# A hybrid decoder layer: the SSD's normed rows are written to a PSUM bank of their own

## The chip, the cores and the metric

The kernel runs on one core of one Trainium2 chip. The metric is the device time of one execution in microseconds (us); lower is better. Five engines work side by side, each through its own instructions in order: TensorE (PE in the profile; its weight loads are PEld), VectorE (DVE), ScalarE (ACT), GpSimd (POOL), and SyncE (SP), which here issues the DMAs. They wait for each other by semaphores.

## The reference

The layer is one decoder block over 2048 tokens of width 1024. Its first half feeds two mixers from one input projection, and the SSD mixer's tail is what the change touches:

```python
proj = u @ w_in[i]
q, k, v, qi, ki, wi, z, xbc, dt = jnp.split(proj, offsets, axis=-1)
attn = sparse_attention(q, k, v, qi, ki, wi, rel_bias)   # top-256 keys per query
ssd = ssd_mixer(z, xbc, dt, conv_w[i], conv_b[i], dt_bias[i], a_log[i], d_skip[i], ssd_norm_w[i])
mix = jnp.concatenate([attn, ssd], axis=-1) @ w_out[i]
h = h + rms_norm(mix, norm_post_mix[i])
f = rms_norm(h, norm_pre_mlp[i]) @ w_mlp_up[i]
f = jnp.square(jax.nn.relu(f)) @ w_mlp_down[i]
h = h + rms_norm(f, norm_post_mlp[i])

# the end of ssd_mixer: y is (tokens, 512), in 2 groups of 256
y = y * jax.nn.silu(z)
yg = y.reshape(Bn, L, 2, 256)
yg = yg * lax.rsqrt(jnp.mean(yg * yg, axis=-1, keepdims=True) + EPS)
y = yg.reshape(Bn, L, 512) * norm_w
```

## The kernel before

Tokens go in four tiles `t` of 512, each of four chunks `c` of 128. Large products are made from high and low parts: each operand is split into a rounded part and a remainder, and `mm3` (L255) issues three matmuls for one (L257, L260, L261). These are the main products: the input projection into `p_mm` (`in_proj`, 21 products of 24 matmuls for each tile), then for each tile the output projection into `p_acc` and the MLP into `p_mm` and `p_dn`.

The program has a front (input projection of the four tiles) and then four windows, one for each tile (output projection and MLP). Beside the main products run the side tasks: the top-k search of the sparse attention (`topk`), the attention itself (`attention`), and the SSD (`ssd`). `weave` (L934) interleaves them in the text by given start and end points, with a priority for each kind. The order on each engine is then made by a scheduler that plays the program through by its own estimates and takes the most urgent instruction that it finds ready; so one added instruction or one other buffer can move what comes after it, on every engine.

`ssd(t)` walks the chunks in order, for two groups `g` of heads in each. `enter(c, g)` loads the tile `si` (three buffers), transposes it into `p_x` (L496, L497) and makes the decays `lm` and `cb`: after `p_x` come DVE's L500, ACT's L502 and DVE's L503, and only then can the chunk's matmuls start. `carry` issues these into `p_y` (L514, L515) and `p_st` (L517), and updates the state. `leave(c, sis)` normalizes the two groups of a finished chunk: squares (L530), sums of squares by matmuls into `p_ms` (L532), the reciprocal root on DVE (`rsqrt`), and for each group a matmul that spreads the result over a bank's columns (L538, into the same bank `p_ms`). DVE multiplies it into the rows (L540, two instructions of 128 columns), ACT makes the high part (L542), DVE the low part (L543), and SP stores both to `mix_d`, from which the output projection reads.

A chunk's order in the text is: carry of group 0 (`p_y`, `p_st`), enter of group 1 (`p_x`), carry of group 1 (`p_y`, `p_st`), enter of the next chunk's group 0 (`p_x`), and leave (`p_ms`). For the first three tiles these take turns on two PSUM banks, `acc` and `acd` (`rings["acc"]`, L100): each call of `pt` takes the other bank, and waits until the earlier tile in it is done with. The transposes and spreads of the input projection (`p_tr` at L341 and L422, `p_rs` at L288) take turns on the same two. The fourth tile's SSD uses the three banks `tp`, which it shares with top-k and attention.

Of the kernel before, what the change touches and what calls it, by code (L numbers as in the profile page):

```python
# [8 lines left out]
F32 = mybir.dt.float32  # L9
# [6 lines left out]
AF = mybir.ActivationFunctionType  # L16
OP = mybir.AluOpType
# [24 lines left out]
def hybrid_layer(ctx, tc, x, x_t, w_cols, n_post_mix, n_post_mlp, w_in, w_misc, dt_bias, a_log, d_skip,  # L42
                 w_out, w_up, w_down, rel_bias, c_ident, c_flip, c_stack, c_tri, c_trineg, c_caus, c_bucket, out, dbg=None):
    nc = tc.nc
    V, S, G, PE, SP = nc.vector, nc.scalar, nc.gpsimd, nc.tensor, nc.sync
# [56 lines left out]
    def pt(tag, name=None):  # L102
        pool, bufs, slot = place(tag)
        return pool.tile([P, 512], F32, tag=slot, name=name or tag, bufs=bufs)
# [27 lines left out]
    w_pm, w_pl, w_ssd = cols[:, 0:8], cols[:, 8:16], cols[:, 56:60]  # L132
# [69 lines left out]
    def rsqrt(o, v, n, scale, who="s", work=None, also=None):  # L202


        if work is None:
            xx, u = (tl(who, [P, n], name=name) for name in ("rs_x", "rs_u"))
        else:
            xx, u = work[:, 0:n], work[:, n:2 * n]
        yi = tl(who, [P, n], I32, name="rs_y")
        V.tensor_scalar(xx, v, scale, EPS, op0=OP.mult, op1=OP.add)  # L210
        if also is not None:
            V.scalar_tensor_tensor(xx, also, scale, xx, op0=OP.mult, op1=OP.add)
        V.tensor_scalar(yi, xx.bitcast(I32), -0.5, float(0x5f3759df), op0=OP.mult, op1=OP.add)
        y = yi.bitcast(F32)
        q = tl(who, [P, n], name="rs_q")

        V.tensor_tensor(u, xx, y, op=OP.mult)
        V.tensor_tensor(u, u, y, op=OP.mult)
        V.tensor_scalar(q, u, 0.375, -1.25, op0=OP.mult, op1=OP.add)
        V.tensor_tensor(u, u, q, op=OP.mult)  # L220
        V.scalar_tensor_tensor(y, u, 1.875, y, op0=OP.add, op1=OP.mult)

        V.tensor_tensor(u, xx, y, op=OP.mult)
        V.scalar_tensor_tensor(u, u, -0.5, y, op0=OP.mult, op1=OP.mult)
        V.scalar_tensor_tensor(o, u, 1.5, y, op0=OP.add, op1=OP.mult)
# [232 lines left out]
    def ssd(t):  # L458
        bank = "acc" if t < NT - 1 else "tp"
# [65 lines left out]
        def leave(c, sis):  # L525

            p = pt(bank, "p_ms")
            for g, si in enumerate(sis):
                ys, sq = si[:, 0:2], si[:, 2:4]
                S.activation(sq, ys, AF.Square)  # L530
                for j in range(2):
                    PE.matmul(p[:, g:g + 1], sq[:, j], cn["ones"], start=j == 0, stop=j == 1)  # L532
            rs = tl("ssm", [P, 2], name="rs_s")
            rsqrt(rs, p[:, 0:2], 2, 1.0 / 256, "ssm", p[:, 2:6])
            for g, si in enumerate(sis):
                ys, yp = si[:, 0:2], si[:, 2:6].rearrange("p (s j) t -> p s j t", s=2).bitcast(F32R)
                sl = slice((g + 1) * P, (g + 2) * P)
                PE.matmul(p[:, sl], rs[:, g:g + 1].broadcast_to([P, P]), ident, start=True, stop=True)  # L538
                for j in range(2):
                    V.scalar_tensor_tensor(ys[:, j], ys[:, j], w_ssd[:, 2 * g + j:2 * g + j + 1], p[:, sl],  # L540
                                           op0=OP.mult, op1=OP.mult)
                S.activation(yp[:, 0], ys, AF.Copy)  # L542
                V.tensor_tensor(yp[:, 1], ys, yp[:, 0].bitcast(F32), op=OP.subtract)  # L543
                r0, t0 = 512 + 256 * g, t * T + c * P
                for s in range(2):
                    SP.dma_start(mix_d[s, r0:r0 + 256, t0:t0 + P].rearrange("(j p) t -> p j t", p=P), yp[:, s].bitcast(F32))
# [541 lines left out]
```

## Time and profile before

| | |
|---|---|
| three runs | 2923.69, 2925.88, 2927.11 us; median 2925.88 us |
| the profiled execution | 2928.29 us, its span 2926.5 us |
| share of the span that an engine is busy | PE 94%, POOL 60%, DVE 56%, ACT 51% |
| mean granted TensorE clock | 0.973 of full speed |
| the front, 0 to 895 us | PE busy 789.28 us of 895, granted clock 0.94 |
| the rest, 895 to 2926 us | PE busy 1972.61 us of 2031, granted clock 0.99 |

How to read it: a busy PE is not PE at its peak, since matmuls overlap; but an idle PE is time in which it had nothing that it could start. The granted clock is the share of full speed that TensorE was given. The SSD's leaves lie between 189 and 881 us, so all that the change edits runs in the front and at the start of the first window.

### The profile page before, as it was taken

The page shows a single profiled execution, that of the slowest core. Times are in us where ns is not written, and L with a number is a line of the kernel's source. Part 1 is how long each engine was busy: PE and PEld are TensorE (multiplying, and loading weights), DVE is VectorE, ACT ScalarE, POOL GpSimd, SP SyncE. Part 2 cuts the span into 40 slices and gives each one's busy share as a digit, 9 for nine tenths or more (in the row PEclk, how much of TensorE's full clock was granted, in tenths as well). Part 3 has the DMA queues.
Part 4 walks back from the last instruction along what each step waited for, and adds up shares of the span by engine and source line. Part 5 has one row for each costly group of instructions (what it writes and reads, how often), then busy time and mean ns, then how long its engine had stood idle before and what let it go on. Part 6 is the DMA issues. An engine that isn't in the chain of part 4 may idle for free.

```text
span 2926.5 us, 41201 instructions
## 1 busy us (share of the span) xinstructions
PE 2761.9 (94%) x13558; PEld 2250.7 (77%) x13558; DVE 1642.4 (56%) x4106; ACT 1481.5 (51%) x2550; POOL 1762.6 (60%) x1721
## 2 busy tenths in 40 slices
PE   7988989789989999998999999999999999999998
PEld 5766767667768887887787888878888888778886
DVE  5479588888575666747765565666444342511113
ACT  2375477675837575677773847644332332311101
POOL 4666556667666656654456575644564656588775
PEclk8999989999989999999999999999999999999999
DMA  3765654634733333255223222553222225522222
GB/s 128 224 189 151 218 157 149 208 118 160 249 120 119 112 103 102 90 176 180 101 94 98 90 97 79 170 177 102 87 95 81 93 78 177 204 95 97 95 94 86
DMA packets 286741, 383.46 MB, mean 131 GB/s; under 512 B 26520, under 2 KB 151360, under 8 KB 286528
## 3 DMA queue, kind: packets, MB, share of 16 engines
q1 hardware_dynamic: 286528, 380.84, 40.0%
q8 instruction: 107, 1.75, 0.2%
q14 instruction: 106, 0.87, 0.1%
HBM read 316.44 MB, written 64.30 MB: 130 GB/s over the span
## 4 chain that ended last, share of the span: by engine, by line
PE 67%; DVE 13%; ACT 6%; DMA 5%; issue 4%; POOL 3%; SPq 1%; POOLq 0%; DVEq 0%; ACTq 0%
PE p_mm L257 9%; PE p_mm L261 9%; PE p_mm L260 9%; PE p_dn L260 7%; PE p_dn L261 7%; PE p_dn L257 7%; ACT junk_k L610 5%; PE p_o L725 4%; PE p_s L683 4%; PE p_pt L717 3%; POOL wl L232 2%; PE p_ix L591 1%; DVE cnd L618 1%; PE p_acc L260 1%; PE p_acc L257 1%
## 5 line engine op out<-in xcount | busy, mean ns | idle before, releaser
L232 POOL TENSOR_TENSOR wl<-wr,wh 128x512 fp32r<-128x512 f32 (+1 forms) x740 | 987.0, 1335 | 179.6 <-ACT wh L229 107.0
L231 POOL TENSOR_SCALAR wh<-wr 128x512 fp32r<-128x512 f32 x674 | 449.6, 667 | 752.1 <-PE p_mm L260 372.8
L257 PE MATMUL p_mm<-u,wh 128*128 128x512 f32 (+1 forms) x1696 | 685.4, 404 | 47.4 <-ACT u L311 15.4
L261 PE MATMUL p_mm<-u,wl 128*128 128x512 f32 (+1 forms) x1696 | 682.8, 404 | 13.2 <-POOL wl L232 12.9
L260 PE MATMUL p_mm<-u,wh 128*128 128x512 f32 (+1 forms) x1696 | 674.9, 398 | 0.6 <-POOL u L309 0.3
L610 ACT ACTIVATE junk_k<-sc,cnd 128x512 int8<-128x512 f32 (+10 forms) x434 | 576.4, 1328 | 157.8 <-DVE cnd L618 122.2
L257 PEld LDWEIGHTS p_mm<-u,wh 128*128 128x128 f32 (+1 forms) x1696 | 322.9, 190 | 119.3 <-ACT u L311 17.5
L260 PE MATMUL p_dn<-wl,g 128*128 128x512 f32 x1008 | 402.2, 399 | 4.2 <-POOL wl L232 4.2
L261 PE MATMUL p_dn<-wh,g 128*128 128x512 f32 x1008 | 399.5, 397 | 2.7 <-POOL g L836 2.7
L261 PEld LDWEIGHTS p_mm<-u,wl 128*128 128x128 f32 (+1 forms) x1696 | 322.5, 190 | 88.7 <-POOL wl L232 21.3
L260 PEld LDWEIGHTS p_mm<-u,wh 128*128 128x128 f32 (+1 forms) x1696 | 322.6, 190 | 69.6 <-DVE u L312 2.3
L257 PE MATMUL p_dn<-wh,g 128*128 128x512 f32 x1008 | 328.0, 398 | 1.9 <-POOL wh L231 1.3
L834 ACT ACTIVATE r<-r 128x512 f32<-128x512 f32 x128 | 80.4, 629 | 437.1 <-DVE r L833 436.7
L688 DVE CUSTOM_DVE_ANT_0 pp<-p_s,mk 128x512 f32<-128x512 f32 (+3 forms) x320 | 192.5, 607 | 134.3 <-PE p_s L683 130.5
L719 ACT ACTIVATE ppt<-p_pt 128x512 fp32r<-128x512 f32 (+1 forms) x288 | 155.3, 568 | 208.1 <-PE p_pt L717 170.0
L720 DVE TENSOR_TENSOR ppt<-p_pt,ppt 128x512 fp32r<-128x512 f32 (+1 forms) x288 | 182.6, 655 | 129.6 <-ACT ppt L719 126.9
L260 PEld LDWEIGHTS p_dn<-wl,g 128*128 128x128 f32 x1008 | 190.3, 189 | 46.8 <-POOL wl L232 5.5
L261 PEld LDWEIGHTS p_dn<-wh,g 128*128 128x128 f32 x1008 | 190.3, 189 | 43.8 <-POOL g L836 3.1
L257 PEld LDWEIGHTS p_dn<-wh,g 128*128 128x128 f32 x1008 | 185.8, 189 | 42.0 <-POOL wh L231 2.9
L725 PE MATMUL p_o<-ppt,VV 128*128 128x256 f32 x1088 | 211.1, 294 | 1.9 <-DVE ppt L720 1.0
L617 DVE TENSOR_SCALAR keep<-cnt 128x1 int32<-128x1 f32 (+1 forms) x341 | 70.2, 206 | 244.1 <-ACT junk_k L610 242.7
L836 POOL TENSOR_TENSOR g<-r,g 128x512 fp32r<-128x512 f32 x128 | 170.1, 1331 | 53.2 <-ACT g L835 51.9
(253 smaller groups left out, 4177.6 us busy)
## 6 DMA issues: line engine op xcount, KB each, us to landing
wr<-w_up SPq DMA_DIRECT2D x256, 256.0 KB, 2.6
wr<-w_down SPq DMA_DIRECT2D x256, 256.0 KB, 2.6
wr<-w_in SPq DMA_DIRECT2D x160, 256.0 KB, 2.9
tq<-toep_d SPq DMA_DIRECT2D x128, 128.0 KB, 2.6
qs<-q_d SPq DMA_DIRECT2D x256, 64.0 KB, 2.5
wr<-w_out SPq DMA_DIRECT2D x64, 256.0 KB, 3.7
mix<-mix_d SPq DMA_DIRECT2D x32, 512.0 KB, 8.1
q_d<-qp SPq DMA_DIRECT2D x24, 512.0 KB, 3.6
```

Source lines behind the costliest of these rows:

```text
L231: G.tensor_scalar(dst_hi, src_f, 1.0, 0.0, op0=OP.mult, op1=OP.add)
L232: G.tensor_tensor(dst_lo, src_f, dst_hi.bitcast(F32), op=OP.subtract)
L257: m = PE.matmul(o, ah, bh, start=first, stop=False)
L260: PE.matmul(o, ah, bl, start=False, stop=False)
L261: state["mm3"] = PE.matmul(o, al, bh, start=False, stop=last).ins.name
L610: S.activation(junk_k[:, 0:n], scs[j], AF.Sign, bias=bias(j), accum_out=cnt[:, j:j + 1])
L683: PE.matmul(p[:, 0:w], qs[:, var, hh, :], K1[:, g, j0:j0 + w], start=var == 0, stop=var == 1)
L688: V.tensor_tensor_reduce(out=pp[:, j0:j0 + w], in0=p[:, 0:w], in1=mk[:, j0:j0 + w], scale=1.0, scalar=-3e38, op0=OP.add, op1=OP.max, accum ...
L719: S.activation(pg[:, 0, 0:w], p[:, 0:w], AF.Copy)
L720: V.tensor_tensor(pg[:, 1, 0:w], p[:, 0:w], pg[:, 0, 0:w].bitcast(F32), op=OP.subtract)
L725: PE.matmul(po[:, c0:c0 + 256], VV[:, kk, g, :], pg[:, part, j * 256:(j + 1) * 256], start=kk == 0 and part == 0, stop=kk == nb - 1 and pa ...
L836: G.tensor_tensor(gt[:, 1, :], r, gt[:, 0, :].bitcast(F32), op=OP.subtract)
```

## The change

The product of L540 no longer goes back into the `si` tile in SBUF. It goes into a new tile `p_ys` in a PSUM bank of its own, taken from the same ring as `p_ms`, and the high and low parts are made from there. No instruction is added or removed on any engine: only operands, the ring's turns and, through these, the order change. Lines from L541 on have numbers two higher in the changed kernel, and L536 to L539 one higher.

```diff
             rs = tl("ssm", [P, 2], name="rs_s")
             rsqrt(rs, p[:, 0:2], 2, 1.0 / 256, "ssm", p[:, 2:6])
+            p2 = pt(bank, "p_ys")
             for g, si in enumerate(sis):
                 ys, yp = si[:, 0:2], si[:, 2:6].rearrange("p (s j) t -> p s j t", s=2).bitcast(F32R)
                 sl = slice((g + 1) * P, (g + 2) * P)
                 PE.matmul(p[:, sl], rs[:, g:g + 1].broadcast_to([P, P]), ident, start=True, stop=True)
+                yn = p2[:, g * 256:(g + 1) * 256].rearrange("p (j t) -> p j t", j=2)
                 for j in range(2):
-                    V.scalar_tensor_tensor(ys[:, j], ys[:, j], w_ssd[:, 2 * g + j:2 * g + j + 1], p[:, sl],
+                    V.scalar_tensor_tensor(yn[:, j], ys[:, j], w_ssd[:, 2 * g + j:2 * g + j + 1], p[:, sl],
                                            op0=OP.mult, op1=OP.mult)
-                S.activation(yp[:, 0], ys, AF.Copy)
-                V.tensor_tensor(yp[:, 1], ys, yp[:, 0].bitcast(F32), op=OP.subtract)
+                S.activation(yp[:, 0], yn, AF.Copy)
+                V.tensor_tensor(yp[:, 1], yn, yp[:, 0].bitcast(F32), op=OP.subtract)
```

A chunk now takes eight turns on the two banks instead of seven. On PE the same 647 instructions come first in both; from there (the SSD's first chunk, some 190 us into the run) the order differs on every engine up to the last window, whose order is the same. Three places show it.

On DVE, the second half of the first leave in before, with what each row waits for (names in front of the arrow are the tile written; `p_ms` is the spread root, `si` the rows):

```order
L543 TENSOR_TENSOR si<-si 128x256 [waits Activation_49]
L374 SCALAR_TENSOR_TENSOR p_mm<-raw,cols,p_mm 128x512 [waits DVE_49]
L224 SCALAR_TENSOR_TENSOR rs_u<-rs_u,rs_y 128x4 [waits DVE_49]
L453 TENSOR_SCALAR sp_r<-sp_r 128x32 [waits DVE_49]
L617 TENSOR_SCALAR keep<-cnt 128x2 [waits Activation_49]
L540 SCALAR_TENSOR_TENSOR si<-si,cols,p_ms 128x128 [waits PE_49,Pool_49]
L540 SCALAR_TENSOR_TENSOR si<-si,cols,p_ms 128x128
```

The same leave on DVE in the changed kernel:

```order
L542 SCALAR_TENSOR_TENSOR p_ys<-si,cols,p_ms 128x128 [waits PE_49]
L542 SCALAR_TENSOR_TENSOR p_ys<-si,cols,p_ms 128x128 [waits DVE_49]
L722 TENSOR_TENSOR ppt<-p_pt,ppt 128x256 [waits Activation_49]
L619 TENSOR_SCALAR keep<-cnt 128x2 [waits Activation_49]
L620 SCALAR_TENSOR_TENSOR cnd<-keep,cnd 128x2 [waits DVE_49]
L545 TENSOR_TENSOR si<-p_ys,si 128x256 [waits Activation_49]
L542 SCALAR_TENSOR_TENSOR p_ys<-si,cols,p_ms 128x128 [waits DVE_49,PE_49,Pool_49]
```

The second product of a pair now waits for the first (32 pairs), and the second group's products wait for the first group's low part, since both groups write one bank.

On PE, the first chunk of the third tile's SSD in before (`p_y`, `p_x`, `p_y` of its two groups, after 1512 main matmuls):

```order
L514 MATMUL p_y<-lm,xd 64x128
L515 MATMUL p_y<-cb,st 64x128
L496 MATMUL p_x<-ident,si 128x128 x3
L497 MATMUL p_x<-si 128x128
L514 MATMUL p_y<-lm,xd 64x128
```

The same transposes on PE in the changed kernel:

```order
L260 MATMUL p_mm<-u,wh 76x512
L261 MATMUL p_mm<-u,wl 76x512
L496 MATMUL p_x<-ident,si 128x128 x3
L497 MATMUL p_x<-si 128x128
L257 MATMUL p_mm<-u,wh 76x512
L260 MATMUL p_mm<-u,wh 76x512
```

Twelve main matmuls now lie ahead of these transposes, and twelve behind them, before the second group's `p_y`.

On PE, the leave of that chunk in before, after 1560 main matmuls (the second L538 comes twelve main matmuls behind the rows shown, and the next `p_y` another ten after it):

```order
L261 MATMUL p_mm<-u,wl 128x512
L538 MATMUL p_ms<-ident,rs_s 128x128
L257 MATMUL p_mm<-u,wh 128x512
L260 MATMUL p_mm<-u,wh 128x512
L517 MATMUL p_st<-xd 128x256
L261 MATMUL p_mm<-u,wl 128x512
```

The same leave on PE in the changed kernel, after 1584 main matmuls (L539 is the spread; `p_tr` is the input projection's transpose of the misc columns), with the start of the `p_y` behind it:

```order
L261 MATMUL p_mm<-u,wl 128x512
L539 MATMUL p_ms<-ident,rs_s 128x128 x2
L343 MATMUL p_tr<-ident,mi 128x76 x4
L517 MATMUL p_st<-xd 128x256
L514 MATMUL p_y<-lm,xd 64x128
L515 MATMUL p_y<-cb,st 64x128
```

and the end of that same `p_y`, directly behind it the transposes and the next group's `p_y`:

```order
L515 MATMUL p_y<-cb,st 64x128
L496 MATMUL p_x<-ident,si 128x128 x3
L497 MATMUL p_x<-si 128x128
L514 MATMUL p_y<-lm,xd 64x128
L515 MATMUL p_y<-cb,st 64x128
```

Here no main matmul is left between the spread, `p_tr`, `p_st`, `p_y`, `p_x` and the second `p_y`, where in before 24 and more lie between each two.

## Rows read from the trace of the kernel before

**Rows 1.** The page: engines' busy time, share and instructions.

```profile
PE 2761.9 (94%) x13558; PEld 2250.7 (77%) x13558; DVE 1642.4 (56%) x4106; ACT 1481.5 (51%) x2550; POOL 1762.6 (60%) x1721
```

**Rows 2.** Busy time by stretch (start:end, length, engines; granted clock, DMA share, GB/s).

```profile
0.00:895.00 895.00, 789.28 (x3900) 619.37 (x3901) 648.47 (x1713) 533.69 (x1099) 550.91 (x562) 0.94 0.54 172
895.00:2926.00 2031.00, 1972.61 (x9660) 1631.33 (x9658) 993.94 (x2393) 947.82 (x1452) 1211.71 (x1160) 0.99 0.34 113
```

**Rows 3.** Groups by line and form: busy us, mean ns | idle before, releaser.

```profile
L374 DVE SCALAR_TENSOR_TENSOR p_mm<-raw,cols,p_mm 128x512 f32<-128x512 f32 x64 | 47.9, 748 | 2.0 <-ACT p_mm L372 1.6
L374 DVE SCALAR_TENSOR_TENSOR pre<-raw,cols,p_mm 128x512 f32<-128x512 f32 x32 | 23.6, 739 | 0.4
L543 DVE TENSOR_TENSOR si<-si 128x256 fp32r<-128x256 f32 x32 | 21.3, 666 | 2.5 <-ACT si L542 2.5
L540 DVE SCALAR_TENSOR_TENSOR si<-si,cols,p_ms 128x128 f32<-128x128 f32 x64 | 19.4, 337 | 5.4 <-PE p_ms L538 5.4
L720 DVE TENSOR_TENSOR ppt<-p_pt,ppt 128x256 fp32r<-128x256 f32 x32 | 13.3, 417 | 12.4 <-ACT ppt L719 12.2
...
L542 ACT ACTIVATE si<-si 128x256 fp32r<-128x256 f32 x32 | 13.1, 409 | 24.7 <-DVE si L540 24.6
L719 ACT ACTIVATE ppt<-p_pt 128x256 fp32r<-128x256 f32 x32 | 11.9, 373 | 24.6 <-PE p_pt L717 18.4 <-PE p_o L725 6.3
```

**Rows 4.** Timeline (start, length) of L540, L543 and POOL; L543's ns min/median/max.

```profile
202.07 0.59 DVE L540 SCALAR_TENSOR_TENSOR si<-si,cols,p_ms 128x128 f32<-128x128 f32 x2
...
L543 DVE TENSOR_TENSOR si<-si x32: 406/419/1555, 205.1 to 879.9; 128x256 fp32r<-128x256 f32 x32
...
732.51 1.55 DVE L543 TENSOR_TENSOR si<-si 128x256 fp32r<-128x256 f32 x1
...
732.49 1.30 POOL L232 TENSOR_TENSOR wl<-wr,wh 128x512 fp32r<-128x512 f32 x1
```

**Rows 5.** Timeline of PE, 570 to 587 us: start, length, records [idle before].

```profile
569.98 0.39 PE L260 MATMUL p_mm<-u,wh 128*128 128x512 f32 x1
570.21 0.39 PE L261 MATMUL p_mm<-u,wl 128*128 128x512 f32 x1
573.62 0.55 PE L514 MATMUL p_y<-lm,xd 128*64 128x128 f32 x2 [3.02 <-DVE ends L492]
...
578.18 0.52 PE L496 MATMUL p_x<-ident,si 128*128 128x128 f32 x3 [0.95 <-PE p_y L515]
...
583.68 0.88 PE L514 MATMUL p_y<-lm,xd 128*64 128x128 f32 x4 [4.76 <-DVE lm L503]
...
586.43 0.99 PE L257 MATMUL p_mm<-u,wh 128*76 128x512 f32 x1
```

**Rows 6.** Timeline of PE, 623 to 635 us.

```profile
623.16 0.45 PE L514 MATMUL p_y<-lm,xd 128*64 128x128 f32 x4
...
623.87 0.44 PE L515 MATMUL p_y<-cb,st 128*64 128x128 f32 x4
...
629.08 0.88 PE L496 MATMUL p_x<-ident,si 128*128 128x128 f32 x3 [1.94 <-issue]
...
632.67 1.87 PE L532 MATMUL p_ms<-ones,si 128*128 128x1 f32 x8 [2.07 <-DVE st L519]
634.78 0.76 PE L257 MATMUL p_mm<-u,wh 128*128 128x512 f32 x1 [0.24 <-DVE p_ms L210]
```

**Rows 7.** Timeline of PE, 814 to 825 us.

```profile
814.48 0.38 PE L538 MATMUL p_ms<-ident,rs_s 128*128 128x128 f32 x2
820.17 0.87 PE L496 MATMUL p_x<-ident,si 128*128 128x128 f32 x3 [5.31 <-DMA si<-s_d]
...
824.73 0.70 PE L514 MATMUL p_y<-lm,xd 128*64 128x128 f32 x4 [3.27 <-DVE lm L503]
```

**Rows 8.** Busy time by stretch, around the second of those places.

```profile
626.00:636.00 10.00, 5.34 (x20) 4.21 (x20) 8.41 (x25) 7.89 (x17) 4.35 (x5) 0.62 0.13 46
```

**Rows 9.** Timeline of PE: a `p_y` that waited for the normed rows.

```profile
207.09 0.45 PE L514 MATMUL p_y<-lm,xd 128*64 128x128 f32 x4 [1.21 <-DVE si L540]
```

## The prediction

> **What bounds the kernel now.** I read first the busy times of the page, then the stretches, then the stretches' PE timeline. PE is busy 94% of the span, no other engine above 60% [rows 1], so an edit counts by what it does to PE's standing still and to PE's clock, not by what it does to the engine that it edits. The stretches show where there is something to win or lose: up to 895 us PE is idle 895 - 789.28 = 105.7 us and the granted clock is 0.94; over the following 2031 us it is idle 58.4 us at 0.99 [rows 2]. The leaves that the change edits lie in the first of these. There PE's idle time is not one large wait but some fifty of 0.3 to 5 us, and the two or three largest clusters belong to the SSD: the reader sees them in the PE timeline as `p_x` and `p_y` one behind the other, with no main matmul between them [rows 5 to 7].
>
> **The edited operations.** The low part, L543, has a median of 419 ns and a mean of 666, with a longest of 1555 [rows 3, 4]. The long ones go beside POOL: the one at 732.51 starts 0.02 us after a POOL subtraction of 1.30 us, and ends at 734.06, 0.27 us after that [rows 4]. A DVE step of the same size with one operand in PSUM and one in SBUF, L720 on 256 columns, takes 417 ns on average over 32 [rows 3]. I take that: 32 x (666 - 417) = 8.0 us less of DVE. The two ends are 0 (the long ones stay) and 8.3 us (all at 406). [...]
>
> The product, L540, now writes PSUM. The nearest pair is L374, 748 ns into PSUM against 739 into SBUF [rows 3]: 64 x 0.009 = 0.6 us more. The second of each pair now waits for the first; two steps of 337 ns took 0.59 us together without that [rows 3, 4], so at most 0.08 us each, 32 x 0.08 = 2.6 us. The high part reads PSUM: ACT's L719 on 256 columns takes 373 ns against 409 for L542 [rows 3], 32 x 0.036 = 1.2 us less of ACT. Together DVE is freed of 8.0 - 0.6 - 2.6 = 4.8 us and ACT of 1.2 us. No instruction of the trace waited for L543 on another engine; what it delays is only the work queued behind it on DVE. DVE is busy 72% of the first 895 us (648.47 us) [rows 2], and PE's idle share there is 12%. As an estimate from these, a fifth to a quarter of DVE time that is freed shows on PE: I take 1 us, between 0 and 4.8.
>
> [...]
>
> **The bank.** A chunk takes eight turns on two banks instead of seven. `p_ms` and `p_ys` now hold both banks during a leave, so the next `p_y` cannot start before L540 has read `p_ms`, or before the low parts have read `p_ys`. In before `p_y` could go ahead and only `p_st` had to wait. The scheduler knows this and sets `p_y` behind the spread everywhere; what is left open is whether it leaves enough main matmuls between. Main matmuls start 0.23 us apart [rows 5]. In most chunks 20 to 50 of them lie between spread and `p_y`, 4.6 to 11 us. The chain that they must hide is two products, ACT, the low part, two products, ACT, the low part: 2 x (0.67 + 0.37 + 0.41) = 2.9 us by the rows [rows 3], some 4 us with the semaphores between. Those cost nothing, as long as DVE and ACT are not far behind.
>
> **What goes.** Three places of before come apart. First, the third tile's first chunk [rows 5]. `p_y` waits 3.02 us, `p_x` 0.95, the second `p_y` 4.76, and the next main matmul starts at 586.43. The first wait stays. From 577.23 (where `p_x` could have started) to 586.43 are 9.2 us. The work in them at full clock is one `p_y` of 1.15 us (623.16 to 624.31 [rows 6]), one `p_st` and one `p_x` of about 0.9 us together, so 9.2 - 2.05 = 7.2 us go. Twelve main matmuls on each side of `p_x`, 5.5 us, cover the 5.5 us from `p_x` to `p_y` (583.68 - 578.18). Second, 623 to 635 us [rows 6]: from 624.31 to 634.78 are 10.5 us with about 2.7 us of work, so 7.8 us. In the change `p_cs`, `p_x`, `p_st` and `p_ms` there lie 10 or more main matmuls apart. Third, the wait for `si` at 820 us [rows 7]: 5.31 us between the spread and `p_x`. Twelve `p_acc` matmuls now stand between, 12 x 0.23 = 2.8 us. The `p_y` behind it keeps its 3.27 us. Sum: 7.2 + 7.8 + 2.8 = 17.8 us less. [...]
>
> **What comes.** The worst new place is after 1584 main matmuls, where spread, `p_tr`, `p_st`, `p_y`, `p_x` and `p_y` follow each other. By the rows: two spreads 0.3, two products 0.67, ACT 0.37, low part 0.41, two products 0.67, `p_tr` 0.4, its copy on DVE 0.4, `p_st` 0.35, `p_y` 1.15, L521 0.6 (its reader, before `p_x` gets the bank), `p_x` 0.55, then 4 us to the next `p_y` (4.76 and 3.27 [rows 5, 7]), and 1.15: 11.0 us, of which 3.9 are work. That is 7 us; with eight semaphores and the slower clock that such a stretch had [rows 8] I take 10, between 7 and 13. Two smaller ones, after 576 and 1080 main matmuls: ten short side matmuls, some 1.3 us, lie between `p_x` and `p_y`, so of the 3.27 to 4.76 us about 2 to 3.5 remain; with the clock 3.8 each, 7.6 together. Sum: 17.6 us more.
>
> **The sum.** 17.6 - 17.8 - 1 = -1.2 us against the profiled execution of 2928.29 us, which lies 2.4 us above the median of the three runs, 2925.88. The forecast is 2925.88 - 1.2 = 2924.7 us. What I could not price is the rest of the order. The other waits of the front (some 60 us, of attention, top-k and the weights' split) and the 58.4 us behind 895 us [rows 2] meet another order too, up to the last window. The work in them is the same, and up to 2000 main matmuls the same count of side matmuls lies ahead of the same main matmul; so this moves waits about, and I see no sign. A reshuffle of some fifty waits of about 2 us each moves their sum by 10 to 15 us either way.
>
> **The rivals.** *Faster:* the three places come apart as reckoned, and the new ones are hidden, since freed DVE and ACT time lets `lm` and the normed rows be ready sooner. For it: DVE was the releaser of most of these waits [rows 5, 6], and it has 4.8 us less to do. Against it: nothing in the order lies between the rows at 1584. It gives 2925.88 - 17.8 - 1 = 2907 us; with half of the new ones, 2916. *Slower:* the leave on PE's path. One `p_y` of before waited 1.21 us for the products of a leave [rows 9], where it was placed too early; in the change every chunk's first `p_y` stands behind them. If DVE or ACT run late enough that the 2.9 us chain takes more than the 20 main matmuls (4.6 us) that the tightest of these have, each of 16 leaves costs 1.2 us and more. That is 19 us with 1.2 each, so 2925 + 19 = 2944 us. It decides where the queue ahead of L540 or L543 holds more than 1.7 us. *Not as it says:* the long L543 stay, because their other operand is still in SBUF; then the 8.0 us are not freed, DVE gets 3.2 us more, and the time is about 2927 us. Its chance is small, 0.05, since L720 has the same form and no such length.
>
> **How the numbers follow.** Two times within 0.2% of 2925.88 us (2920 to 2931.7) cannot be told apart by a measurement of this kernel; that is "same". Forecast, near zero: 0.31, and with the third rival 0.36. Faster, 2907 to 2919: 0.34. Slower, 2932 to 2944 and above: 0.30. The faster and slower cases hold most of the chance together, so the likeliest case has its own range, 2920 to 2931.7. The range for 8 in 10 reaches to both: 2907 less 6 us of unpriced order below, 2944 with the same above, 2901 to 2950.
>
> **What would show it.** In the profile of the changed kernel: L545 with a mean near 417 ns and no instruction over 0.7 us (the freed DVE time); the `p_x` near 580 us and the one near 630 with waits under 1 us (what goes); a `p_y` with 3 to 5 us of idle near 600 us, behind `p_tr`, and PE busy under 6 us in ten there (what comes); PE's busy time before 895 us within 5 us of 789. It would be wrong if the idle time behind 895 us moved by more than 10 us, since I count nothing there, or if `p_y` waited for the normed rows in most leaves.

## The result: 35 us slower, in two places

The changed kernel takes 2961.77 us (median of 2955.32 to 2965.74) against 2926.49 us (2923.69 to 2931.19): a ratio of 1.0117, 95% interval 1.0097 to 1.0137. The forecast was 2924.7 us, the range 2901 to 2950; both are wrong. The profiled execution is the fastest of the changed kernel, 2955.32 us, and lies 27.0 us above the profiled one of before, 2928.29. What follows splits these 27 us; the other 8 lie between a profiled execution and its kernel's median and can't be placed. The ratios here and below are of fast runs; one execution of before (3083 us) and one of e5 (12958 us) stand outside them.

First the page's row of engines, in the kernel after (compare [rows 1]):

```profile
PE 2769.4 (94%) x13558; PEld 2254.3 (76%) x13558; DVE 1630.5 (55%) x4106; ACT 1480.5 (50%) x2550; POOL 1768.7 (60%) x1721
```

VectorE is busy 11.9 us less, 5.0 of them in the edited lines (below), and TensorE 7.5 us more with the same 13558 instructions. The stretches of [rows 2], in the kernel after (start:end, length, busy time of PE, PEld, DVE, ACT and POOL with instructions, granted clock, DMA share, GB/s):

```profile
0.00:895.00 895.00, 778.53 (x3826) 611.46 (x3827) 627.67 (x1691) 525.82 (x1083) 544.36 (x550) 0.93 0.53 170
895.00:2953.00 2058.00, 1990.89 (x9734) 1642.80 (x9732) 1002.85 (x2415) 954.71 (x1467) 1224.29 (x1172) 0.99 0.35 112
```

A cut at a fixed time puts other work on each side of it, since 74 instructions of TensorE have slipped behind 895 us. So I cut by work: the main matmuls (L257, L260, L261) are counted in TensorE's timeline, and a stretch goes from the first TensorE instruction behind one count to the first behind another. Three cuts are enough: **start** is up to main 504, **front** from 504 to 2400 (all leaves lie in it, and the SSD is over at its end), **windows** from 2400 to 7392. Behind that both kernels take the same 382 us. The stretches front, windows and end in TensorE's rows, first of the kernel before, then of the kernel after (start:end, length, PE busy, clock, DMA share, GB/s):

```profile
164.00:897.00 733.00, 652.14 (x3347) 0.94 0.53 170
897.00:2544.00 1647.00, 1604.34 (x8075) 0.99 0.35 116
2544.00:2926.00 382.00, 366.27 (x1576) 0.98 0.29 102
```

```profile
160.00:912.00 752.00, 658.48 (x3341) 0.92 0.52 165
912.00:2572.00 1660.00, 1609.25 (x8081) 0.99 0.36 115
2572.00:2953.00 381.00, 364.64 (x1576) 0.99 0.30 101
```

By the timeline the start takes 164.0 us before and 159.5 after (-4.5), the front 732.9 and 752.5 (+19.6), the windows 1647.4 and 1659.6 (+12.2); the end gives back the 0.3 us over 27.0. In the front about two thirds of the 20 us is idle time, 733 - 652.14 = 80.9 us against 93.5, and a third is longer busy time, at a granted clock of 0.92 of full speed in place of 0.94. The windows hold no step of the SSD, and still lose 12 us.

Next the edited operations, as groups by line in the kernel after (busy us, mean ns | idle before, releaser), and below them the shortest, median and longest of the low part, L545:

```profile
L542 DVE SCALAR_TENSOR_TENSOR p_ys<-si,cols,p_ms 128x128 f32<-128x128 f32 x64 | 22.3, 348 | 2.5 <-PE p_ms L539 1.8
L545 DVE TENSOR_TENSOR si<-p_ys,si 128x256 fp32r<-128x256 f32 x32 | 13.4, 418 | 5.8 <-ACT si L544 5.6
L544 ACT ACTIVATE si<-p_ys 128x256 fp32r<-128x256 f32 x32 | 12.1, 377 | 31.2 <-DVE p_ys L542 29.4 <-DVE cnd L615 1.2 <-DVE cnd L620 0.6
```

```profile
L545 DVE TENSOR_TENSOR si<-p_ys,si x32: 393/418/426, 197.3 to 890.7; 128x256 fp32r<-128x256 f32 x32
```

The low part fell from a mean of 666 to 418 ns and its longest from 1555 to 426 [rows 3, 4]. The change does to these instructions what it was priced at, and the time goes the other way.

### The profile page after: what moved, and what is told of

Same layout as the page of the kernel before. It is cut to its first block, busy times and chain, and to the rows that moved or that the text cites. A ratio compares the mean times of both kernels' runs of the same rounds, so it can differ in the third digit from the quotient of the medians.

```text
span 2953.5 us, 41225 instructions
## 1 busy us (share of the span) xinstructions
PE 2769.4 (94%) x13558; PEld 2254.3 (76%) x13558; DVE 1630.5 (55%) x4106; ACT 1480.5 (50%) x2550; POOL 1768.7 (60%) x1721
## 4 chain that ended last, share of the span: by engine, by line
PE 61%; DVE 11%; ACT 7%; DMA 4%; issue 4%; POOL 3%; SPq 0%; POOLq 0%; DVEq 0%; ACTq 0%
PE p_mm L261 8%; PE p_mm L257 8%; PE p_mm L260 8%; PE p_dn L260 7%; PE p_dn L261 7%; PE p_dn L257 7%; ACT junk_k L612 5%; PE p_s L685 3%; PE p_o L727 3%; PE p_pt L719 3%; PE p_ix L593 1%; PE p_acc L260 1%; PE p_acc L257 1%; POOL wl L232 1%; PE p_acc L261 1%
## 5 line engine op out<-in xcount | busy, mean ns | idle before, releaser
L257 PE MATMUL p_mm<-u,wh 128*128 128x512 f32 (+1 forms) x1696 | 682.6, 403 | 41.1 <-ACT u L311 14.3
L261 PE MATMUL p_mm<-u,wl 128*128 128x512 f32 (+1 forms) x1696 | 681.5, 403 | 13.4 <-POOL wl L232 13.2
L260 PE MATMUL p_mm<-u,wh 128*128 128x512 f32 (+1 forms) x1696 | 672.8, 397 | 0.5 <-POOL u L309 0.3
L257 PEld LDWEIGHTS p_mm<-u,wh 128*128 128x128 f32 (+1 forms) x1696 | 323.1, 191 | 113.5 <-ACT u L311 16.3
L260 PE MATMUL p_dn<-wl,g 128*128 128x512 f32 x1008 | 402.9, 400 | 5.8 <-POOL wl L232 5.8
L261 PE MATMUL p_dn<-wh,g 128*128 128x512 f32 x1008 | 399.9, 397 | 2.8 <-POOL g L838 2.8
L261 PEld LDWEIGHTS p_mm<-u,wl 128*128 128x128 f32 (+1 forms) x1696 | 321.9, 190 | 88.4 <-POOL wl L232 20.4
L260 PEld LDWEIGHTS p_mm<-u,wh 128*128 128x128 f32 (+1 forms) x1696 | 322.1, 190 | 70.5 <-DVE u L312 2.3
L257 PE MATMUL p_dn<-wh,g 128*128 128x512 f32 x1008 | 330.8, 400 | 6.8 <-POOL wh L231 5.6
L260 PEld LDWEIGHTS p_dn<-wl,g 128*128 128x128 f32 x1008 | 190.7, 189 | 49.1 <-POOL wl L232 7.9
L257 PEld LDWEIGHTS p_dn<-wh,g 128*128 128x128 f32 x1008 | 187.4, 190 | 49.0 <-POOL wh L231 9.0
L261 PEld LDWEIGHTS p_dn<-wh,g 128*128 128x128 f32 x1008 | 190.6, 189 | 43.3 <-POOL g L838 3.2
```

The source lines that it names most:

```text
L257: m = PE.matmul(o, ah, bh, start=first, stop=False)
L260: PE.matmul(o, ah, bl, start=False, stop=False)
L261: state["mm3"] = PE.matmul(o, al, bh, start=False, stop=last).ins.name
```

## The experiments

Four theories. **A**: the eighth turn on the PSUM ring costs, by taking both banks for a leave (A': all of it on the ring of two). **B**: the PSUM operands cost. **C**: nothing of the change itself costs; any shift of the side work against the main matmuls moves the time by tens of us, and the kernel before stands at a low spot. **D**, formed later: two prices, one for the twelve leaves of the first three tiles, paid in the front, and one for the last tile's, paid in the windows.

The table has all kernels, by profiled execution (start, front, windows in us as above) and by the median of all runs. SS are the two points of `weave` between which the first tile's SSD is interleaved (L981); the other tiles follow at a fixed distance. Some expectations give the windows by an earlier count, which ended some 14 main matmuls sooner, so that they are 6 to 10 us shorter than here: 1639.6 us for before, which is 1647.4 in the table.

| kernel | SS | start | front | windows | median | ratio to before (95%) |
|---|---|---|---|---|---|---|
| before | 90, 170 | 164.0 | 732.9 | 1647.4 | 2926.5 | 1 |
| after | 90, 170 | 159.5 | 752.5 | 1659.6 | 2961.8 | 1.0117 (1.0097-1.0137) |
| e1: operands only, p_ms's bank | 90, 170 | 164.5 | 742.1 | 1646.3 | 2936.4 | 1.0036 (1.0024-1.0048) |
| e2: turn only | 90, 170 | 163.1 | 768.5 | 1656.1 | 2976.7 | 1.0170 (1.0149-1.0191) |
| e3: turn on the ring of three | 90, 170 | 163.5 | 750.7 | 1671.2 | 2970.9 | 1.0158 (1.0136-1.0180) |
| e5: before | 91, 171 | 164.2 | 749.9 | 1655.4 | 2953.1 | 1.0087 (1.0067-1.0106) |
| e6: after | 91, 171 | 161.3 | 772.3 | 1664.2 | 2981.6 | 1.0180 (1.0145-1.0214) |
| e9: p_ms's bank | 91, 171 | 161.9 | 743.8 | 1682.1 | 2971.4 | 1.0153 (1.0119-1.0186) |
| e7: before | 89, 169 | 162.4 | 746.1 | 1643.4 | 2935.4 | 1.0028 (1.0010-1.0046) |
| e8: after | 89, 169 | 161.8 | 753.0 | 1663.9 | 2966.6 | 1.0130 (1.0095-1.0165) |
| e14: before | 88, 168 | 165.3 | 750.5 | 1644.0 | 2944.0 | 1.0071 (1.0044-1.0098) |
| e15: after | 88, 168 | 162.6 | 749.9 | 1660.8 | 2961.8 | 1.0135 (1.0099-1.0172) |
| e16: p_ms's bank | 88, 168 | 166.9 | 745.6 | 1646.1 | 2943.2 | 1.0071 (1.0045-1.0098) |
| e17: p_ms's bank | 90, 165 | 164.2 | 749.1 | 1645.1 | 2940.0 | 1.0049 (1.0033-1.0065) |
| e10: own bank in tiles 0-2, p_ms's in tile 3 | 90, 170 | 163.0 | 752.6 | 1644.2 | 2951.9 | 1.0083 (1.0061-1.0106) |
| e11: p_ms's bank in tiles 0-2, own in tile 3 | 90, 170 | 159.1 | 742.8 | 1656.7 | 2944.5 | 1.0066 (1.0045-1.0087) |
| e12: before in tiles 0-2, own bank in tile 3 | 90, 170 | 164.2 | 737.8 | 1656.4 | 2940.8 | 1.0047 (1.0029-1.0065) |
| e13: before in tiles 0-2, p_ms's bank in tile 3 | 90, 170 | 165.3 | 732.6 | 1656.7 | 2940.7 | 1.0048 (1.0030-1.0066) |

### Operands or turn

**e1**: the PSUM operands without the turn. The normed rows overwrite p_ms, in an order in which no row is overwritten before it is read.

```diff
-            p2 = pt(bank, "p_ys")
-                yn = p2[:, g * 256:(g + 1) * 256].rearrange("p (j t) -> p j t", j=2)
-                for j in range(2):
+                yn = p[:, g * 256:(g + 1) * 256].rearrange("p (j t) -> p j t", j=2)
+                for j in ((0, 1), (1, 0))[g]:
```

> The PSUM operands are kept and the bank is taken away: the two normed rows overwrite p_ms itself, each in the place of its own squares and spread, so that a leave has one turn on the ring of two banks again, as in the kernel before, and the steps stand on TensorE almost where they stood before. Theory A (the eighth turn costs: a leave occupies both banks in a row, and leave after leave stands against p_x and p_y): the loss of 35 us goes and the cheaper subtractions stay, 2918 to 2928 us; L540/L544-like groups as in the changed kernel (subtraction 0.42 us, not 0.67). Theory B (the PSUM operands cost, through the second scalar_tensor_tensor and an ACT that starts later): the loss stays, 2950 us or more. Theory C (any shift of the side work against the main matmuls moves the time by tens of us): the order is nearly that of before, so 2926 within 8 us, with the waits of TensorE at 580 and 630 us back where they were.

Measured 2936.4 us, 10 above before. Its low part, in the groups by line of this kernel, costs what the changed kernel's does:

```profile
L544 DVE TENSOR_TENSOR si<-p_ms,si 128x256 fp32r<-128x256 f32 x32 | 13.4, 418 | 4.6 <-ACT si L543 4.5
```

B's 2950 fails and so does A's 2928, and C's 2934 by 2 us. Without the turn 25 of the 35 us are gone, the windows' part among them (1646.3 us, against 1647.4 before), but the front keeps 9.2 us.

**e2**: the turn without the operands. The spreads of a leave get a bank of their own after the rsqrt.

```diff
-            p2 = pt(bank, "p_ys")
+            p = pt(bank, "p_sp")
```

(and L540 to L543 as in before).

> The bank alone: the operands are in SBUF as before (subtraction 0.67 us), but the two spreads of a leave are written into a bank of their own, taken after the rsqrt, so that a leave has two turns on the ring. Theory A (the turn costs): 2950 to 2970 us, the loss of the changed kernel and some of the 8 us of VectorE on top. Theory B (the operands cost): 2926 us within 8. Theory C (any shift of the order): somewhere else again, 2915 to 2965, with the losses in other stages than those of the changed kernel.

Measured 2976.7 us, above A's interval and C's; B, which expected 2926, falls for good. The low part is long again:

```profile
L544 DVE TENSOR_TENSOR si<-si 128x256 fp32r<-128x256 f32 x32 | 21.9, 683 | 1.9 <-ACT si L543 1.8
```

With the turn, this kernel loses 35.6 us in the front, and the changed kernel only 19.6. So the cheaper operands may well give something back; but the orders differ too, and what part of the 16 us is theirs isn't shown.

**e3**: the bank p_ys from the attention's ring of three.

```diff
-            p2 = pt(bank, "p_ys")
+            p2 = pt("tp", "p_ys")
```

> The changed kernel with p_ys taken from the ring of three banks on which the attention has its transposes and scores, so that the ring of two has seven turns again per pair of steps. Theory A: if it is the turn on the ring of two that costs, most of the loss goes: 2920 to 2938 us, with the waits on p_x and p_y near 580 and 630 us no longer than before. If a leave's second turn costs wherever it stands, it stays at 2950 or above, with waits on p_s and p_pt of the attention in place of those on p_x and p_y. Theory B (operands): 2955 to 2965. Theory C: anything from 2915 to 2965.

Measured 2970.9 us: the front's loss is hardly smaller (17.8 us), the windows' is twice as large (23.8). A in its first form, that seven turns on the ring of two would cure it, falls. That a turn costs wherever it stands agrees with it, but isn't shown by this one order.

### What a mere shift is worth

**e5** changes no instruction, only two numbers of `weave`.

```diff
-    SS = (90,170)
+    SS = (91,171)
```

> The kernel before with one number changed: the SSD's tiles are due one step later (91 and 171 in place of 90 and 170), which moves some side steps by a few main matmuls and leaves every instruction as it is. It measures what a mere shift of the side work is worth. Theories A and B: 2926 us within 6. Theory C: it moves by 10 us or more either way, as the table of due times was picked with the old order.

Measured 2953.1 us: 27 us slower for one unit. A and B, which said 2926 within 6, have nothing for this; C expected a move of 10 us or more. The front loses 17.0 us, nearly as much as by the change, and the windows 8.0. After this no single comparison at one order can price the change, and the next runs put it against its partner at other due times.

> The changed kernel with the SSD due one step later (91 and 171), to stand against the kernel before with the same due times, 2953 us. Theory A (the eighth turn has a price of its own, whatever the order): 20 to 45 us above that, 2973 to 2998. Theory C (the 35 us are those of one order against another, the change itself is worth little): within 15 us of 2953 on either side, 2938 to 2968, and it may as well be the faster of the two.

> The kernel before with the SSD due one step earlier (89 and 169). Theory A: no statement, it is the partner of the next run. Theory C: 10 to 40 us above 2926, like the shift the other way (2953), as the due times of the kernel before are a low spot for its own order; within 5 us of 2926 would speak against a low spot.

> The changed kernel with the SSD due one step earlier. Theory A: 20 to 45 us above the kernel before with the same due times. Theory C: within 15 us of it on either side; and against 2962 of the changed kernel itself it moves by 10 us or more, as the kernel before did.

> The normed rows in the bank of p_ms (no turn more, operands in PSUM) with the SSD due one step later. It stands between the kernel before and the changed kernel with the same due times. Theory A: 5 to 15 us below the kernel before at 2953, since only the cheaper subtraction is left. Theory B (the PSUM operands cost): 10 us or more above 2953, as it was 10 above at the old due times. Theory C: anything from 2930 to 2975.

> The kernel before with the SSD due two steps earlier (88 and 168). If the old due times are a low spot of the old order alone, 2932 to 2955 us; if the shift of one step later (2953) was the exception, within 8 us of 2927. The windows have the order of the kernel before, so any loss stands before main 2400.

> The changed kernel with the SSD due two steps earlier. If the turn has a price of its own (A), 20 us or more above the kernel before with the same due times, some 8 to 17 of it in the windows, whose order is again of the slower kind; if the order is all (C), the front may come out on either side of its partner and only the windows' 8 to 17 remain.

> The normed rows in p_ms's bank with the SSD due two steps earlier. The windows have the order of the kernel before, so nothing is lost there (1637 to 1640 us). A: between 5 us faster and 10 us slower than the kernel before with the same due times. C: anywhere within 20 us of it.

> The normed rows in p_ms's bank, with the SSD's tiles due from 90 to 165 in place of 170: each tile is spread over fewer steps and ends earlier. The windows' order is of the faster kind from main 5700 on. If the form without a turn can keep what the subtractions give, 2918 to 2927 us; if the earlier end piles side work against the SSD, 2930 to 2950.

(e6, e8 and e15 are the changed kernel, e7 and e14 the kernel before, e9, e16 and e17 the kernel of e1, each with SS as in the table and nothing else changed.)

After minus before, by medians, at the due times 88, 89, 90 and 91: 17.8, 31.1, 35.3 and 28.5 us, 28 on average. It is slower at each of the four, and e6 and e8 lie in A's interval of 20 to 45 us and outside C's of 15, so C in its pure form falls there. e15 is 2 us under A's and fits C as it was put for that run: the front on a level with its partner's, and a loss in the windows alone. And before alone goes from 2926.5 to 2944.0, 2935.4 and 2953.1, so 90 is a low spot of its order by 9 to 27 us (e7's 9 us are just under the 10 that C asked for), while after moves less, 2961.8 to 2981.6. Without the pair at 90 the average is 26 us. By stretch the two parts behave differently. Windows: +16.8, +20.5, +12.2, +8.8, always slower, 15 on average. Front: -0.6, +6.9, +19.6, +22.4, 12 on average, with so wide a spread that four pairs don't settle its size. The rows in p_ms's bank, against before at 88, 90 and 91, take -0.8, +9.9 and +18.3 us; e16 lies in A's interval and in C's; e9 lies where B had it, but its front is 6.1 us shorter than its partner's and its windows 26.7 us longer, and the windows have no leave. For the operands these three show no price that holds from one order to the next. For the turn, after lies above the form without it by 18.6, 25.4 and 10.2 us at 88, 90 and 91. e17 looked for a due time at which that form beats before, and didn't find one: 2940.0, in the upper of its two ranges.

### First three tiles or last

The last tile's SSD has its banks in the attention's ring of three, the other three in the ring of two (L459). So the leaves can be changed apart.

This is e10; e11 has `bank == "tp"` in the condition.

```diff
-            p2 = pt(bank, "p_ys")
+            p2 = pt(bank, "p_ys") if bank == "acc" else p
...
-                for j in range(2):
+                for j in ((0, 1), (1, 0))[g]:
```

> The changed kernel up to the last tile: the twelve leaves of the first three tiles take the bank p_ys from the ring of two, the four leaves of the last tile put the normed rows into p_ms's own bank, so that the attention's ring of three has no turn more. TensorE's order is that of the changed kernel for the first 2016 main matmuls, and that of the kernel before again in the windows. Theory D (two prices: the twelve leaves cost some 15 us in the front, and the four turns on the attention's ring another 12 us, which show only behind 895 us, where the order of the windows is another): 2938 to 2946 us, with the front's 15 us there and the windows back at 1639.6 us from main 2400 to 7392. Theory A' (the whole loss is the two-bank ring's, and the windows only pass it on): 2955 to 2963. Theory C: no statement.

> The other half: the leaves of the first three tiles put their normed rows into p_ms's bank (no turn more), the four leaves of the last tile take p_ys from the attention's ring of three. Theory D: 8 to 12 us in the front, as in the kernel with all leaves in p_ms's bank, and 8 to 14 us in the windows: 2942 to 2952. Theory A': 2936, like the kernel with all leaves in p_ms's bank.

e10: front 752.6, as in the changed kernel (752.5); windows 1644.2, as in the kernel before (1647.4) or better. Its median of 2951.9 us lies between the intervals of D (to 2946) and A' (from 2955); only its profiled execution, the fastest of four at 2943.9, is in D's. e11: front 742.8, as in e1 (742.1); windows 1656.7. Its 2944.5 us is in D's interval and not in A'. So in these two the front's loss goes with the first three tiles' leaves, and the windows' with a bank of their own for the last tile's; the next two show that the bank isn't needed for it.

This is e12; e13 has `p2 = p`, with j in e1's order for the last tile.

```diff
-            p2 = pt(bank, "p_ys")
+            p2 = pt(bank, "p_ys") if t == NT - 1 else p
-                yn = p2[:, g * 256:(g + 1) * 256].rearrange("p (j t) -> p j t", j=2)
+                yn = ys if t < NT - 1 else p2[:, g * 256:(g + 1) * 256].rearrange("p (j t) -> p j t", j=2)
```

> The kernel before for the first three tiles, operands and order alike; the last tile's four leaves as in the changed kernel, with p_ys from the attention's ring. The first 2016 main matmuls should take the 753 us of before. Theory D: the four turns cost 8 to 15 us, nearly all of it behind 895 us: 2934 to 2942. Theory A' or B: 2926 within 5 (four leaves of 2 us of VectorE saved each).

> The kernel before for the first three tiles; the last tile's four leaves write the normed rows into p_ms's bank: no turn more anywhere, only the operands of four leaves in PSUM. The order of the main and side work in the windows comes out as in the changed kernel near main 7000 all the same. Theory D in its narrow form (the turns on the attention's ring are the price): 2926 within 5. If the order of the windows is the price, whatever brought it about: 5 to 12 us behind 895 us, 2931 to 2938.

e12 takes 2940.8 us, in D's interval, with 9.0 us lost in the windows and 4.9 in the front, where D had put next to nothing. e13 decides whether the windows need the turn: it has no turn more anywhere, its front is that of before to 0.3 us, and it still loses 9.3 us in the windows. D's narrow form (2926 within 5) falls; the other expectation has the windows right, and its 2938 is 3 us under the 2940.7 measured. In rows: TensorE's front and windows of e10, then of e13.

```profile
163.00:916.00 753.00, 663.04 (x3349) 0.92 0.53 166
916.00:2560.00 1644.00, 1601.56 (x8073) 0.99 0.37 116
```

```profile
165.00:898.00 733.00, 649.65 (x3341) 0.94 0.54 169
898.00:2555.00 1657.00, 1605.36 (x8082) 0.99 0.37 115
```

The waits show the difference. First the timeline of PE in the windows of the kernel after, then of e13: the same waits at the same steps, to a few hundredths of a us.

```profile
1125.33 0.62 PE L257 MATMUL p_mm<-u,wh 128*128 128x512 f32 x1 [4.53 <-POOL wh L231]
1250.66 0.74 PE L593 MATMUL p_ix<-KI,qi 128*128 128x512 f32 x2 [1.54 <-DVE sc L598]
1554.18 0.50 PE L260 MATMUL p_dn<-wl,g 128*128 128x512 f32 x1 [3.48 <-POOL wl L232]
```

```profile
1111.71 0.80 PE L257 MATMUL p_mm<-u,wh 128*128 128x512 f32 x1 [4.53 <-POOL wh L231]
1237.92 0.74 PE L593 MATMUL p_ix<-KI,qi 128*128 128x512 f32 x2 [1.57 <-DVE sc L598]
1538.76 0.50 PE L260 MATMUL p_dn<-wl,g 128*128 128x512 f32 x1 [3.48 <-POOL wl L232]
```

Then the kernel before, and e10, which share another set:

```profile
1114.96 0.50 PE L257 MATMUL p_mm<-u,wh 128*128 128x512 f32 x1 [1.71 <-POOL wh L231]
1387.28 1.22 PE L591 MATMUL p_ix<-KI,qi 128*128 128x512 f32 x2 [2.83 <-DVE sc L596]
1391.47 1.11 PE L717 MATMUL p_pt<-ident,pp 128*128 128x128 f32 x4 [2.97 <-DVE ppt L720]
```

```profile
1133.55 0.50 PE L257 MATMUL p_mm<-u,wh 128*128 128x512 f32 x1 [1.72 <-POOL wh L231]
1406.08 1.22 PE L593 MATMUL p_ix<-KI,qi 128*128 128x512 f32 x2 [2.83 <-DVE sc L598]
1410.28 1.12 PE L719 MATMUL p_pt<-ident,pp 128*128 128x128 f32 x4 [2.97 <-DVE ppt L722]
```

The windows' time goes with their order, and the scheduler arrives at one of a few. TensorE's order from main 3000 to 3900 tells the kernels apart: before, e1, e7, e10, e14, e16 and e17 have one there, matmul for matmul by tiles and shapes, and their windows take 1643.4 to 1647.4 us. The other eleven have other orders, and theirs take 1655.4 to 1682.1: after, e13 and e15 share one (1656.7 to 1660.8), e11, e12 and e2 another (1656.1 to 1656.7). Of the 12.2 us that after loses in the windows, 8.4 stand between these two counts, where it takes 299.0 us for 290.6 with one matmul fewer; e10, in before's order, takes 290.8, and e13, in after's, 296.6. Further on, from main 5700 to 7400, most of the slower kernels share one order, but after loses nothing there: 537.3 us to main 7392 for 538.3 in before, with 55 side matmuls fewer.

e5 is among the slower kernels without any change of its instructions, and so are all four kernels with the full change. What tips the scheduler to one order or another stays open. The slower orders need no turn, as e13 shows, and the last tile's leaves alone don't decide it either: e1 and e10 have the leaves of e13 in that tile, and the faster order.

## Where the prediction failed, step by step

Three terms of the sum failed. "What comes" was priced at 17.6 us, and its places stood far longer; of "what goes", 17.8 us, only one of three places came in full; and the stretch behind 895 us, set at nothing, lost 12.2 us. The front splits into two parts, each with the same number of TensorE's matmuls before and after to within four. From main 504 to 1512, where two small new places were priced at 7.6 us together, the time rose by 16.1 us, from 409.6 to 425.7. From main 1512 to 2400, where 10 us were to come and 17.8 to go, it rose by 3.6, from 323.3 to 326.9. e10, which has after's order up to main 2016, takes nearly the same times, 425.6 and 327.0.

**The edited operations: right.** L545 has a mean of 418 ns for a priced 417 and no long one, L542 rose by 2.9 us for a priced 3.2, ACT's step takes 377 ns for 373. By these DVE lines 5.0 us are freed (21.3 + 19.4 against 13.4 + 22.3), priced at 4.8. With one operand in PSUM the low part takes 418 ns, against a median of 419 with both in SBUF [rows 4].

**"What goes", 17.8 us: one place of three.** The second place, at main 1632 [rows 6], is gone without a wait over 0.5 us. The wait for `si` of [rows 7] fell from 5.31 to 1.80 us, but main 2160 to 2232 around it takes 47.2 us for 47.1 before: new waits stand beside it, 2.09 us before a main matmul and 1.25 and 1.51 us before transposes. And of the first [rows 5] I had said that its first wait of 3.02 us stays. In the timeline of PE after, it is 6.42:

```profile
578.15 0.39 PE L260 MATMUL p_mm<-u,wh 128*128 128x512 f32 x1
578.38 0.39 PE L261 MATMUL p_mm<-u,wl 128*128 128x512 f32 x1
585.18 0.66 PE L514 MATMUL p_y<-lm,xd 128*64 128x128 f32 x2 [6.42 <-ACT u L308]
588.23 0.48 PE L515 MATMUL p_y<-cb,st 128*64 128x128 f32 x1 [1.24 <-POOL cb L504]
590.90 0.71 PE L257 MATMUL p_mm<-u,wh 128*76 128x512 f32 x1 [0.70 <-POOL wh L231]
```

The main products stand still for 590.90 - 578.38 = 12.5 us, where they stood 586.43 - 570.21 = 16.2 before [rows 5]. That is 3.7 us less, and some 2 us of it are `p_x`, the second `p_y` and its `p_st`, whose work now lies between later main matmuls (2.05 us by the prediction's count): about 1.7 us and not 7.2. One reading of the sum was wrong here without harm: of the twelve main matmuls on each side of `p_x` only those behind it lie between it and the second `p_y`, 2.8 us and not 5.5; that `p_y` started without a wait all the same, at 599.76. The wait grew because the main products ran out earlier against the chain ahead of `p_y`, which begins on DVE with L487, when the DMA of `cb` has landed. DVE's timeline, before and after:

```profile
568.66 0.69 DVE L487 TENSOR_TENSOR lm<-cb,trineg 128x512 f32<-128x512 f32 x1 [1.98 <-DMA cb<-cs_d]
```

```profile
581.30 0.69 DVE L487 TENSOR_TENSOR lm<-cb,trineg 128x512 f32<-128x512 f32 x1 [1.90 <-DMA cb<-cs_d]
```

Before it began 570.21 - 568.66 = 1.5 us ahead of the last main matmul; after, 581.30 - 578.38 = 2.9 us behind it. The order as it stands on TensorE didn't show where that transfer lands.

**"What comes", 17.6 us: mis-sized.** The three new places were found, but not their size. Between two main matmuls at 576, 1080 and 1584, 2.7, 3.9 and 2.6 us passed before, and 18.2, 20.0 and 22.5 after; part of that is side work that stood elsewhere before. The one at main 1584 was priced at 10 us, at most 13. PE there, in the kernel after, and below it the stretch (busy PE, PEld, DVE, ACT, POOL; clock):

```profile
614.70 0.39 PE L261 MATMUL p_mm<-u,wl 128*128 128x512 f32 x1
614.93 0.38 PE L539 MATMUL p_ms<-ident,rs_s 128*128 128x128 f32 x2
620.06 0.51 PE L539 MATMUL p_ms<-ident,rs_s 128*128 128x128 f32 x2 [4.75 <-DVE cnd L620]
621.97 0.74 PE L343 MATMUL p_tr<-ident,mi 76*128 76x76 f32 x4 [1.39 <-DVE p_ys L542]
628.88 0.88 PE L496 MATMUL p_x<-ident,si 128*128 128x128 f32 x3 [2.36 <-DMA si<-s_d]
634.13 0.70 PE L514 MATMUL p_y<-lm,xd 128*64 128x128 f32 x4 [3.95 <-DVE lm L503]
637.17 0.79 PE L257 MATMUL p_mm<-u,wh 128*128 128x512 f32 x1 [1.01 <-DVE pre L374]
```

```profile
615.00:640.00 25.00, 10.88 (x55) 8.01 (x54) 18.69 (x68) 16.84 (x36) 6.85 (x8) 0.61 0.32 95
```

No main matmul starts for 637.17 - 614.70 = 22.5 us, with 3.9 us of work in them by the prediction's count: 18.6 us and not 10. Five of them are a step that the prediction had set aside with "as long as DVE and ACT are not far behind". DVE's timeline there:

```profile
614.18 0.16 DVE L225 SCALAR_TENSOR_TENSOR rs_s<-p_ms,rs_y 128x2 f32<-128x2 f32 x1
615.51 0.17 DVE L619 TENSOR_SCALAR keep<-cnt 128x2 int32<-128x2 f32 x1 [1.18 <-ACT junk_k L612]
615.72 1.23 DVE L620 SCALAR_TENSOR_TENSOR cnd<-keep,cnd 128x2 int32<-128x2 int32 x1
616.86 0.34 DVE L542 SCALAR_TENSOR_TENSOR p_ys<-si,cols,p_ms 128x128 f32<-128x128 f32 x1
619.58 0.17 DVE L619 TENSOR_SCALAR keep<-cnt 128x2 int32<-128x2 f32 x1 [2.38 <-ACT junk_k L612]
619.66 0.35 DVE L542 SCALAR_TENSOR_TENSOR p_ys<-si,cols,p_ms 128x128 f32<-128x128 f32 x1
```

The second product stands behind the top-k's count test, which waits 2.38 us for ACT, and the second spread starts when that product has ended (619.66 + 0.35 = 620.01 and 620.06). The prediction added up the leave's own chain and left out what stands between its instructions in DVE's queue. The wait of `p_x` for its DMA, 2.36 us, was not in it either. The 3 us that the prediction had added for eight semaphores and a slower clock were an estimate, and no row priced a semaphore; over these 25 us the granted clock is 0.61 of full speed. The smaller places, at 576 and 1080, were priced at 3.8 us each for the step from `p_x` to `p_y`, with the clock in it. At 576 the waits stand elsewhere, before `p_x`, before attention's matmuls behind it (`p_s`) and further on. PE there, in the kernel after, from the last main matmul to the next:

```profile
199.67 0.40 PE L261 MATMUL p_mm<-u,wl 128*128 128x512 f32 x1
204.49 0.52 PE L496 MATMUL p_x<-ident,si 128*128 128x128 f32 x3 [1.10 <-DVE sp_e L442]
207.23 0.69 PE L685 MATMUL p_s<-K,qs 128*128 128x256 f32 x2 [1.67 <-DVE mx L690]
209.94 0.79 PE L685 MATMUL p_s<-K,qs 128*128 128x256 f32 x2 [2.01 <-DVE atp L755]
217.88 0.77 PE L257 MATMUL p_mm<-u,wh 128*128 128x512 f32 x1
```

The waits at 576 sum to 6.5 us (1.2 before the change), at a granted clock of 0.70 over 200 to 218 us. Those at 1080 sum to 5.7 us, the larger ones 0.65 to 2.55 us each, and at main 1128 another 7.1 us follow, the last of them 4.44 us before a main matmul, where before had 1.94. What the side matmuls at these places wait for, the attention's and the top-k's own steps on DVE, was not in the sum.

**"Behind 895 us nothing": wrong by 12 us.** I wrote that the order there moves waits about and that I see no sign. The runs show a sign for this change: all four pairs lost 9 to 21 us in the windows. The test that I had named for it, idle time behind 895 us moving by over 10 us, stood at 67.1 - 58.4 = 8.7 and so didn't fire; cut by work the loss is 12.2, of which some 8 are idle. The other test, PE busy before 895 us within 5 us of 789, failed, with 778.53.

**The rivals.** "Slower" had the right sign but not the mechanism, and its 19 us are the front's 19.6 by chance. Its condition, a queue of more than 1.7 us ahead of the products, was met at 1584; but it needed `p_y` to wait for the normed rows in most leaves. Of the idle time before L514 (matmuls and their weight loads) in the kernel before and then after, by releaser (us, times):

```profile
  DVE si L540: 5.6, 4
```

```profile
  DVE si L545: 0.5, 2
```

The wait that it rested on [rows 9] has all but gone. What was lost was lost at other places of the order, not at each leave. "Faster" falls too: DVE's freed time didn't hide the new places, as 1584 shows. "Not as it says" is ruled out by L545. A reading was off too: the front of before has 67 waits over 0.3 us and not some fifty, and the two longest, 7.0 and 6.4 us, stand at its very start, before the SSD.

## What to carry to other kernels

One buffer turn more, in a kernel whose order a scheduler makes, is priced by the order that comes out and not by the five microseconds of engine time that the edit saves: here the saving of engine time came as forecast, and the time still rose by 35 us. Before such an edit is judged, put both versions at a few neighbouring due times; at 88 to 91 the kernel before alone ranged over 27 us, and only the pairs, 18 to 35 us apart, showed that the change is slower at more than one order. In a chain that must be hidden, add up the queue of the engine between the chain's instructions, with the waits of the other tasks' instructions in it, and not the chain alone; and don't set a stretch at nothing because no edited instruction lies in it.

## What the runs showed beyond that

TensorE's order up to main 504 is the same, instruction for instruction, in fifteen of the eighteen kernels of the table (all but those at 88, 168), and this stretch takes 159.1 to 165.3 us. So the 4.5 us that the changed kernel gains there aren't its own: e1 and e11 have the same order to main 2016 and differ by 5.4 us in the start. The low part with one operand in PSUM is free of the long cases in every run that has it, 416 to 423 ns on average and 427 at most, where e2, with both in SBUF again, has 683 on average and 1527 at most. All eleven of before's that took over 500 ns overlap an instruction on POOL, and so do 12 of the 21 others, each 0.41 to 0.42 us long; what makes eleven of them long isn't shown.
